# A DoRA forward pass on one core: the end of the first load phase in small pieces, the first stores one chunk earlier, the first block's load in three parts

## The chip, the core and the metric

The kernel runs on one core of one Trainium2 chip. The metric is the device time of one execution in microseconds, taken as the median of several runs; less is better. The profile is that of one further execution. Its engines are called PE (TensorE, matrix products; PEld is its weight load), DVE (VectorE), ACT (ScalarE), POOL (GpSimd) and SP (SyncE, which here only issues DMAs and waits). Data are moved between the chip's large memory (HBM) and the on-chip memory (SBUF) by 16 DMA engines, which work for all queues. SP's DMAs appear as queue q1, ACT's as q10.

## The reference, cut to what matters

```python
batch, seq_len, in_dim, out_dim = 16, 2048, 256, 256      # rank = 16
W_adapted = W + scale * (lora_A @ lora_B)
W_norm = np.sqrt(np.sum(W_adapted ** 2, axis=0, keepdims=True) + 1e-8)
W_final = W_adapted / W_norm * m
y = x.reshape(-1, in_dim) @ W_final                       # 32768 x 256 times 256 x 256
```

The small matrix W_final is made once. The large part is 32,768 rows of x, read as 33.5 MB in float32, multiplied by it, and written as 33.5 MB in float32.

## The kernel before

**Tiling.** The rows are cut into 8 blocks of 4,096 rows (4 MB). In a block each of the 128 partitions holds 32 neighbouring rows, 32 KB in one piece of HBM. A block has 8 chunks of 512 rows (4 rows per partition), 64 chunks in all, numbered g = 0 to 63; two chunks make a pair p = 0 to 31. "Rows 8 to 15 of block 0" are those of each partition: chunks 2 and 3, that is pair 1. There are five buffers for x of a block each (`XBUFS`). The result of a chunk is written over its own x, so a buffer is free for block b + 5 once block b is stored.

**A pair's way.** POOL rounds the pair from float32 to bf16 (`xb`, line 192). PE transposes it by eight products with the identity (line 297, `turned`). DVE copies the transposed pair out of PSUM (`xt`, line 233). PE multiplies by `w_final` in two groups of eight products, one group for each chunk (line 311, `product`). ACT copies each chunk's result into the place of its x (line 251) and, when a store is due, drains and issues it (lines 254 to 260). Semaphores carry these steps: `rounded`, `turned`, `copied`, `room`, `product`. POOL keeps two `xb` buffers, so the cast of pair p waits until pair p - 2 is transposed.

**The beginning.** Before the loop, PE, DVE and ACT make `w_final` from W, A, B and m; the last steps are two products on DVE for `wam` (line 223), a reciprocal (line 226), and two products for `w_final` (line 229). PE transposes pair 0 ahead of it and then waits for `w_final` (line 322).

**Loads.** SP issues them in the order of the list `loads` of (first chunk, number of chunks), line 104: chunks 0 and 1, chunks 2 to 7, then whole blocks 1 to 6, then block 7 in two halves. Each has its semaphore. POOL waits for a pair's load where it differs from that of the pair before (line 182). The first five blocks go at once. Ahead of block 5, SP waits for stores 0, 1 and 2 (lines 159 to 163; `HALF` is 2), ahead of the last half for store 3.

**Stores.** ACT issues them in the order of the list `stores` of (first chunk, number of chunks, chunk after which it is due), lines 112 to 118. Stores 0 and 1 are blocks 0 and 1, due after chunks 22 and 23. Stores 2 and 3 are the halves of block 2, both due after chunk 24. Then come four stores of one chunk each (chunks 24 to 27, due after chunk 27), in which each partition has only 4 KB in one piece. The remaining stores are due after chunk 47 or later.

**The pause.** At pair 15 (`REST`) POOL waits for store 2, line 188, and so all engines behind it stand still while the first stores run. So the order of the large transfers is: loads of five blocks; stores of blocks 0 to 2; loads of blocks 5 to 7, beside the four stores of one chunk; stores of the rest.

Of the kernel before, what the change touches and what calls it, by code (L numbers as in the profile page):

```python
# [11 lines left out]
def kernel(  # L12
# [10 lines left out]
    nc = tc.nc  # L23
# [19 lines left out]
    XBUFS = 5  # L43
    CH = DJ // J
# [56 lines left out]

    units = [(b * CH, CH) for b in range(NBLK - 1)]
    units += [(NCH - CH, CH // 2), (NCH - CH // 2, CH // 2)]
    loads = [(0, 2), (2, CH - 2)] + units[1:]
    load_of = {g: n for n, (g0, cnt) in enumerate(loads) for g in range(g0, g0 + cnt)}


# [1 line left out]

    F = NBLK - XBUFS  # L110
    G = F * CH
    stores = [(b * CH, CH, 22 + b) for b in range(F - 1)]
    stores += [(G - CH, CH // 2, 24), (G - CH // 2, CH // 2, 24)]
    FIRST = len(stores)
    stores += [(G + c, 1, G + 3) for c in range(4)]
# [9 lines left out]
    def sem(name):  # L125
        if name not in sems:
            sems[name] = tc.alloc_semaphore(name)
        return sems[name]
# [50 lines left out]
    ).then_inc(sem("ident"), 1)  # L179
    for p in range(NPR):  # L180
        b, c = divmod(p, PRB)
        if p == 0 or load_of[2 * p - 1] != load_of[2 * p]:
            nc.gpsimd.wait_ge(sem(f"load{load_of[2 * p]}"), 16)
        if p == 0:


            nc.gpsimd.wait_ge(sem("dve"), 4)
        if p == REST:
            nc.gpsimd.wait_ge(sem(f"store{HALF}"), 16)
        if p >= NXB:  # L190
            nc.gpsimd.wait_ge(sem("turned"), p - NXB + 1)
        nc.gpsimd.tensor_copy(  # L192
            out=xb_bufs[p % NXB][:],
            in_=x_bufs[b % XBUFS][:, 2 * c * J : 2 * (c + 1) * J, :],
        ).then_inc(sem("rounded"), 1)
# [51 lines left out]
    for g in range(NCH):  # L247
        b, c = divmod(g, CH)
# [123 lines left out]
```

## Time and profile before

| what | value |
|---|---|
| median of 7 runs | 164.45 us (162.94 to 165.58) |
| time of the profiled execution | 164.19 us |
| its span, first to last instruction | 162.9 us |
| PE busy | 95.7 us (59% of the span) |
| ACT, POOL, DVE busy | 63.9, 63.0, 47.8 us |
| moved by DMA | 67.42 MB, mean 414 GB/s over the span |
| store 0 issued | 51.95 us |
| pair 15's cast after the pause | 78.44 us |
| last store issued | 133.58 us |

The profile has a row of 40 slices for each engine and for the DMA engines, a row for each queue with its share of the 16 engines' time, groups of instructions with their mean length and what ended the idle time before them, and the DMA issues with the time to landing. Stretches of the span can be asked for on their own; they give each engine's busy time, the granted clock, the DMA engines' busy share and their rate. A packet is counted whole in the stretch in which it starts, so in short stretches the share can be over 1.

### The profile page before, as it was taken

How to read it: one execution, taken by the hardware profiler on the slowest of the kernel's cores; microseconds unless marked ns; L12 is line 12 of the kernel's file. 1: busy time of each engine (PE TensorE's matmuls, PEld its weight loads, DVE VectorE, ACT ScalarE, POOL GpSimd, SP SyncE). 2: the span in 40 equal slices, each digit the busy share in tenths (PEclk: the TensorE clock that was granted, in tenths of full speed). 3: DMA queues.
4: the chain of work that ended last, by engine and by line, in shares of the span. 5: the costliest groups of instructions: out<-in, count | busy, mean ns of one | idle time of the engine just before them, and what ended most of it. 6: DMA issues, size and time to landing. Idle time of an engine off the chain costs nothing. (4 is left out here: it accounts for less than half of the span.)

```text
span 162.9 us, 2005 instructions
## 1 busy us (share of the span) xinstructions
PE 95.7 (59%) x786; PEld 84.3 (52%) x786; DVE 47.8 (29%) x44; ACT 63.9 (39%) x67; POOL 63.0 (39%) x39
## 2 busy tenths in 40 slices
PE   0292499999999720000299989999999950000000
PEld 0061489999999610000279979989899930000000
DVE  0419644536353500000033635444444400000000
ACT  3010047686867460000026684865876860000000
POOL 1046367677685000000764469298586200000000
PEclk9999999999999996555558999999999998555555
DMA  4999998999988989999999999899999999999996
GB/s 169 451 447 422 459 443 386 499 402 394 507 386 370 402 386 467 428 390 439 398 388 435 419 450 431 371 420 421 374 422 443 459 443 394 445 451 435 394 426 290
DMA packets 3780, 67.42 MB, mean 414 GB/s; under 512 B 561, under 2 KB 578, under 8 KB 1218
## 3 DMA queue, kind: packets, MB, share of 16 engines
q1 hardware_dynamic: 1584, 33.82, 48.9%
q10 hardware_dynamic: 2194, 33.59, 48.8%
q14 instruction: 2, 0.02, 0.0%
HBM read 33.85 MB, written 33.55 MB: 414 GB/s over the span
## 5 line engine op out<-in xcount | busy, mean ns | idle before, releaser
L251 ACT COPY x_sb<-y_ps 128x1024 f32<-128x1024 f32 x64 | 62.0, 1014 | 60.8 <-PE y_ps L311 60.3
L192 POOL CAST xb<-x_sb 128x2048 bf16<-128x2048 f32 x32 | 60.5, 1902 | 62.5 <-DMA out_dram<-x_sb 26.6
L311 PE MATMUL y_ps<-w_final,xt 128*128 128x256 bf16 x512 | 63.8, 279 | 1.9 <-PEq L286 1.8
L233 DVE COPY xt<-xt_ps 128x1024 f32<-128x1024 f32 x32 | 39.2, 1224 | 72.2 <-PE xt_ps L297 72.2
L311 PEld LDWEIGHTS y_ps<-w_final,xt 128*128 128x128 bf16 x512 | 51.1, 100 | 9.2 <-issue 2.6
L297 PE MATMUL xt_ps<-identity,xb 128*128 128x128 f32 x264 | 37.4, 289 | 27.8 <-PEq L286 27.8
L297 PEld LDWEIGHTS xt_ps<-identity,xb 128*128 128x128 f32 x264 | 32.2, 150 | 30.0 <-issue 29.6
L229 DVE TENSOR_TENSOR w_final<-wam,rnorm 128x256 bf16<-128x256 f32 x2 | 3.7, 1872 | 0.0
L278 PE MATMUL y_ps<-sq,ones 128*128 128x256 f32 x4 | 2.1, 674 | 1.6 <-DVE sq L218 1.6
L243 ACT ACTIVATE norm<-y_ps,eps_col 128x256 f32<-128x256 f32 x1 | 0.5, 474 | 6.3 <-PE y_ps L278 6.3
L267 PE MATMUL y_ps<-identity,a_nat 128*16 128x128 f32 x2 | 0.6, 397 | 4.0 <-DMA a_nat<-in_lora_A_dram 4.0
L278 PEld LDWEIGHTS y_ps<-sq,ones 128*128 128x128 f32 x4 | 1.2, 323 | 2.3 <-DVE sq L218 2.1
L241 ACT ACT_TABLE_LOAD x1 | 1.3, 1283 | 2.4 <-issue 2.4
L267 PEld LDWEIGHTS y_ps<-identity,a_nat 128*16 128x16 f32 x2 | 0.1, 88 | 4.0 <-issue 4.0
L198 POOL MEMSET xb<- 128x2048 bf16 x1 | 1.8, 1805 | 0.7 <-PE xt_ps L297 0.7
L226 DVE RECIPROCAL rnorm<-norm 128x256 f32<-128x256 f32 x1 | 1.7, 1747 | 0.0
L209 DVE CAST b_bf<-b_nat 16x256 bf16<-16x256 f32 x1 | 0.3, 281 | 4.0 <-DMA b_nat<-in_lora_B_dram 4.0
L220 DVE COPY m_all<-y_ps 128x256 f32<-128x256 f32 x1 | 0.4, 425 | 3.3 <-PE y_ps L283 3.3
L271 PE MATMUL y_ps<-b_bf,aT 16*128 16x256 bf16 x2 | 0.6, 403 | 1.3 <-DVE aT L211 1.3
L283 PE MATMUL y_ps<-m_row,ones 1*128 1x256 f32 x2 | 1.2, 710 | 0.0
L271 PEld LDWEIGHTS y_ps<-b_bf,aT 16*128 16x128 bf16 x2 | 0.1, 105 | 1.8 <-DVE aT L211 1.8
L214 DVE SCALAR_TENSOR_TENSOR wa<-y_ps,w_nat 128x512 f32<-128x512 f32 x1 | 0.7, 691 | 0.8 <-PE y_ps L271 0.8
(13 smaller groups left out, 3.7 us busy)
## 6 DMA issues: line engine op xcount, KB each, us to landing
x_sb<-in_x_dram SPq DMA_DIRECT2D x6, 4096.0 KB, 28.8
out_dram<-x_sb ACTq DMA_DIRECT2D x5, 4096.0 KB, 21.0
out_dram<-x_sb ACTq DMA_DIRECT2D x5, 2048.0 KB, 29.3
x_sb<-in_x_dram SPq DMA_DIRECT2D x2, 2048.0 KB, 33.6
x_sb<-in_x_dram SPq DMA_DIRECT2D x1, 3072.0 KB, 11.9
out_dram<-x_sb ACTq DMA_DIRECT2D x4, 512.0 KB, 48.3
x_sb<-in_x_dram SPq DMA_DIRECT2D x1, 1024.0 KB, 5.2
w_nat<-in_W_dram SPq DMA_DIRECT2D x1, 256.0 KB, 2.8
```

Source lines behind the costliest of these rows:

```text
L192: nc.gpsimd.tensor_copy(out=xb_bufs[p % NXB][:], in_=x_bufs[b % XBUFS][:, 2 * c * J : 2 * (c + 1) * J, :],).then_inc(sem("rounded"), 1)
L198: nc.gpsimd.memset(xb_bufs[NPR % NXB][:], 0.0).then_inc(sem("rounded"), 1)
L214: nc.vector.scalar_tensor_tensor(out=wa[:], in0=ab_ps, scalar=float(scale), in1=w_nat[:], op0=ALU.mult, op1=ALU.add).then_inc(dv, 1)
L226: nc.vector.reciprocal(out=rnorm[:], in_=norm[:]).then_inc(dv, 1)
L229: i = nc.vector.tensor_mul(out=w_final[:, t], in0=wam[:, t], in1=rnorm[:])
L233: nc.vector.tensor_copy(out=xt_bufs[p % NXT][:].rearrange("p r t -> p (r t)").bitcast(FP32), in_=xt_ps[p % 2][:],).then_inc(sem("copied"), 1)
L241: nc.scalar.activation(out=warm[:], in_=eps_col[:], func=AF.Sqrt)
L251: nc.scalar.copy(out=x_bufs[b % XBUFS][:, c * J : (c + 1) * J, :], in_=y_ps[g % 2][:]).then_inc(sem("room"), 1)
L278: i = nc.tensor.matmul(n2_ps, ones[:], sq[:, t, :], start=(t == 0), stop=(t == KC - 1))
L283: nc.tensor.matmul(mb_ps, ones[0:1, :], m_row[:], start=True, stop=True).then_inc(pe, 1)
L297: i = nc.tensor.transpose(xt_ps[p % 2][:, j * P : (j + 1) * P], xb_bufs[p % NXB][:, j, :].bitcast(FP32), identity[:],)
L311: i = nc.tensor.matmul(y_ps[h][:, j, :], xt_bufs[p % NXT][:, r : r + P, t], w_final[:, t, :], start=(t == 0 and (j % (J // 2)) == 0), stop ...
```

## The change

Three edits. The list of loads is cut differently: the load of chunks 2 to 7 becomes one of chunks 2 and 3 and one of chunks 4 to 7, and block 4, the last of the first five, becomes one load of its first five chunks and three loads of one chunk each (4 KB in one piece for each partition). Stores 0 and 1 are due one chunk earlier, after chunks 21 and 22. POOL's wait for a load is asked for each chunk of a pair instead of for its first chunk alone, since the boundary between two loads now falls inside pair 18 (chunks 36 and 37) and pair 19.

```diff
     units += [(NCH - CH, CH // 2), (NCH - CH // 2, CH // 2)]
-    loads = [(0, 2), (2, CH - 2)] + units[1:]
+    loads = [(0, 2), (2, 2), (4, CH - 4)] + units[1 : XBUFS - 1]
+    loads += [((XBUFS - 1) * CH, CH - 3)]
+    loads += [(XBUFS * CH - 3 + c, 1) for c in range(3)] + units[XBUFS:]
     load_of = {g: n for n, (g0, cnt) in enumerate(loads) for g in range(g0, g0 + cnt)}
...
-    stores = [(b * CH, CH, 22 + b) for b in range(F - 1)]
+    stores = [(b * CH, CH, 21 + b) for b in range(F - 1)]
     stores += [(G - CH, CH // 2, 24), (G - CH // 2, CH // 2, 24)]
...
         b, c = divmod(p, PRB)
-        if p == 0 or load_of[2 * p - 1] != load_of[2 * p]:
-            nc.gpsimd.wait_ge(sem(f"load{load_of[2 * p]}"), 16)
+        for g in (2 * p, 2 * p + 1):
+            if g == 0 or load_of[g - 1] != load_of[g]:
+                nc.gpsimd.wait_ge(sem(f"load{load_of[g]}"), 16)
         if p == 0:
```

Here CH is 8, XBUFS is 5 and F is 3. What is computed, the number of bytes moved and the order of the loads by address stay the same.

## The prediction

> **What bounds the kernel now.** I read the page first: rows 2 and 3, then the DMA-issuing rows, then half-microsecond windows around the places where loads and stores change over. In the first fence the first two lines are the DMA queues of the page (the third number is the share of 16 engines' span), the third is the list of waits for SP, the rest are windows (window, length, busy time of PE, PEld, DVE, ACT, POOL, granted clock, DMA share, GB/s).
>
> ```profile
> q1 hardware_dynamic: 1584, 33.82, 48.9%
> q10 hardware_dynamic: 2194, 33.59, 48.8%
> ...
> SPq L163 <- DMA out_dram<-x_sb: 74.2, 1, 74.2
> ...
> 50.50:51.00 0.50, 0.50 (x7) 0.44 (x6) 0.50 (x1) 0.17 (x1) 0.50 (x1) 1.00 2.13 918
> 51.00:51.50 0.50, 0.50 (x8) 0.45 (x5) 0.18 (x1) 0.50 (x1) 0.50 (x1) 1.00 0.00 0
> 51.50:52.00 0.50, 0.50 (x7) 0.50 (x6) 0.00 (x0) 0.34 (x1) 0.38 (x1) 1.00 0.02 0
> 52.00:52.50 0.50, 0.50 (x7) 0.48 (x6) 0.00 (x0) 0.14 (x1) 0.00 (x0) 1.00 0.00 0
> 52.50:53.00 0.50, 0.50 (x7) 0.45 (x5) 0.43 (x1) 0.50 (x1) 0.00 (x0) 1.00 2.44 1049
> ...
> 52.00:78.00 26.00, 5.22 (x45) 4.13 (x43) 2.45 (x2) 4.97 (x5) 0.00 (x0) 0.70 0.99 422
> 78.00:86.00 8.00, 5.52 (x26) 4.57 (x27) 1.23 (x1) 1.14 (x2) 5.63 (x3) 0.50 0.99 366
> 86.00:112.00 26.00, 25.13 (x227) 22.99 (x226) 11.12 (x10) 18.15 (x19) 16.90 (x10) 0.99 1.01 430
> 112.00:122.00 10.00, 9.78 (x90) 8.78 (x89) 4.81 (x4) 6.81 (x9) 7.33 (x4) 1.00 0.99 397
> 122.00:161.00 39.00, 10.38 (x96) 9.38 (x93) 3.67 (x3) 8.70 (x10) 3.89 (x3) 0.70 1.01 434
> ```
>
> The two queues fill 97.7% of the engines' time, so the kernel is bound by moving 67.4 MB; PE, the busiest engine, has 59%. What can be won is where the engines stand or run slow. A packet is booked where it starts: the 16 packets of 32 KB of 52.50:53.00 take 2.44 x 0.5 = 1.22 us. The last load packets start at 50.4 to 50.9, so they end at 51.6 to 52.1, on average at 51.85; the first store packets start at 52.8 to 53.0. Between loads and stores every DMA engine stands **1.0 us**. The other two changes of direction (78 to 86, 112 to 122) do not stand, but run at 366 and 397 GB/s against 434: 8 x (1 - 366/434) = 1.25 us and 10 x (1 - 397/434) = 0.85 us lost. They already have small stores (4 KB a row) beside large loads.
>
> The next fence is the timeline of DVE, POOL and ACT (start, length, engine, line, operation).
>
> ```profile
> 11.84 0.76 DVE L223 TENSOR_TENSOR wam<-wa,m_all 128x256 f32<-128x256 f32 x2
> 12.51 1.75 DVE L226 RECIPROCAL rnorm<-norm 128x256 f32<-128x256 f32 x1
> 13.76 3.92 POOL L192 CAST xb<-x_sb 128x2048 bf16<-128x2048 f32 x2 [3.67 <-DMA x_sb<-in_x_dram]
> 14.29 3.67 DVE L229 TENSOR_TENSOR w_final<-wam,rnorm 128x256 bf16<-128x256 f32 x2
> ...
> 48.21 1.93 ACT L251 COPY x_sb<-y_ps 128x1024 f32<-128x1024 f32 x2 [0.69 <-PE y_ps L311]
> 50.83 1.01 ACT L251 COPY x_sb<-y_ps 128x1024 f32<-128x1024 f32 x1 [0.69 <-PE y_ps L311]
> 51.95 0.37 ACTq L145 DMA_DIRECT2D out_dram<-x_sb  x1
> ```
>
> The first store leaves at 51.95, after chunk 22 (copies start with chunk 0 at 22.01 and come two per 2.62 us; 48.21 is chunks 20 and 21). 0.90 us later its first packet starts: the gap is that latency, begun as the loads end. The two w_final products take 3.67 us, where the two wam products of the same size took 0.76: each ends 0.28 us after one of the two POOL casts that started at 13.76.
>
> **The change, part by part.**
>
> *Store 0 due at chunk 21, store 1 at 22.* Nothing is added on ACT; two drains and issues move up. Chunk 21 ends at 50.14, and the present distance from copy to issue is 0.11: 50.25 instead of 51.95. ACT's next copy then comes about 0.5 us later, as it does today at 52.36; queued behind it is PE's "room", then pairs up to 14. Nobody needs those soon: POOL waits 26.6 us at pair 15 for store 2, which hides 0.5 us fully. The two half stores of block 2 stay at chunk 24.
>
> *Rows 8 to 15 on their own.* (2, 6) becomes (2, 2) and (4, 4). Pair 1 need no longer wait for the 3 MB that land at 13.7: (0, 2) landed at 1.4 + 5.2 = 6.6, and 1 MB more at 430 GB/s is 2.4 us, so about 9.0. Its cast follows pair 0's (8.20 + 1.89) at 10.1 to 12.0. That catches wam: it would start at 11.84, is held to about 12.3 and costs 0.2. Pair 2 still waits for the rest of block 0 (13.8) and blocks the first w_final product to about 16.0; the second is then free, 0.4: w_final is ready at 16.4 instead of 17.96, **1.5 us earlier**, and with it all PE work up to chunk 29. On the path to the end this is worth nothing beyond the gap: pair 15 is held by stores. It moves store 0 to about 48.7. If wam were also caught twice, or (2, 2) landed after 12, the gain falls towards 0 and store 0 goes at 50.25.
>
> *The last three chunks of block 4 one by one.* Eight packets of 32 KB per engine (8 x 1.22) become eight of 20 KB and 24 of 4 KB. The trace has 4 KB packets only as stores. Two bounds, from the queue view of single windows (packets, MB, share of 16 engines):
>
> ```profile
> q10 hardware_dynamic: 40, 0.11, 54.0%
> ...
> q1 hardware_dynamic: 32, 0.52, 122.2%
> q10 hardware_dynamic: 32, 0.13, 31.8%
> ...
> q10 hardware_dynamic: 120, 1.43, 100.4%
> ```
>
> The first line is 82:83, stores alone: 15 are semaphore writes, one is a 16 KB packet of about 1.2 us, and (0.54 x 16 - 1.2)/24 = 0.31 us each for 4 KB. The next two are 94:95, beside large loads: 0.318 x 16/32 = 0.159 us each. At 0.159 the new split costs 24 x 0.159 - 3/8 x 8 x 1.22 = 0.16, with three more semaphore writes 0.2 us; at 0.31 another 24 x 0.15 = 3.6. Below nothing is excluded, since the bytes are the same. I take 0.2: the rows alongside another queue are the nearer, and loads of small rows ran at full rate even at the start (the 2 KB rows of W filled the engines at about 0.09 us each between 2.5 and 3.0). Splitting block 0 adds eight packets per engine, about 0.06.
>
> A rule speaks against this edit. The Trainium skill, "DMA: Bandwidth & Descriptors", section "Rules for kernel authors", asks for 1 MiB or more per DMA, and the section on the anatomy of a DMA fits 2.0 us + bytes/436 GB/s. With it three loads of 512 KB cost 3 x 3.2 = 9.6 us instead of 3.7: 6 us more, an estimate from that page, and the kernel would be slower by about 5 us. The rows say no: from 86 to 112 four DMAs of 512 KB flow beside loads at 430 GB/s. The fixed part is latency of one DMA, and here many are queued.
>
> *SP and POOL.* SP issues four more loads, 0.43 us median each, 1.7 us together: it ends its first batch near 6 instead of 4.2 and then waits 74.2 us for stores. If that cover were gone, 1.7 us. Block 1's issue moves from 2.1 to about 2.5, its packets not before 13. POOL gets four more waits, for (4, 4) at pair 2 and for chunks 37, 38, 39 at pairs 18 and 19, behind which all later casts queue. Those pairs run at 87 and 90; the small loads land about 30 us before. Cost nothing; were they late, every microsecond would hit PE, ACT and the 112.20 stores.
>
> *Which queue goes first.* The same page, section "Queues, rings and completion order", says that an engine goes round its queues packet by packet. Loads issued at 78.48 should then appear at 79.4; the last line of the fence, 79:83, has store packets only, and the first load packet starts near 83.2, some five 16 KB and three 4 KB packets later. So a newcomer waits for about eight packets already taken in. By the rule store 0 starts at 48.7 + 0.9 = 49.6; by the trace eight packets of 4 KB later, about 1.3 us, at 50.9. The loads run to about 52.1 (51.85 + 0.26), so both close the gap, and I use the trace.
>
> *Sum.* -1.0 (gap) + 0.2 + 0.06 = **-0.74 us**. After this the order is unchanged: stores 0 to 2 end 0.74 earlier, so pair 15's cast (78.44) and block 5's loads (78.48) start near 77.7, and the last store, now due at the end of the 162.9 us span, lands near 162.15. The profiled execution took 164.19 and becomes 163.45; the median of the seven runs is 0.26 above it: 164.45 - 0.74 = **163.7**.
>
> **The rivals.** About 1% is what a measurement of this kernel can tell from no change (1.64 us; the seven runs span 2.6).
>
> - *Gap closed as above*, chance 0.46: 163.7, its own range 162.5 to 164.9, from a standing time between 0.6 and 1.4 and the spread of the runs.
> - *More than the gap of this execution*, 0.24. How long w_final is held depends on which of DVE and POOL starts first, and the first store moves with it, so slower executions may stand longer than 1.0. The new order has over 3 us in hand. Then the median falls to the two fastest runs (about 163.0) less 0.74: 162.3. For it: runs of 162.94 and 163.06; against: one profile can't show it.
> - *The mixing costs what the standing did*, 0.15. The two existing changeovers lose 0.85 and 1.25 us without standing. Then -0.74 + 1.05 = +0.3: 164.8. Against: between 86 and 112 the mixture ran at 430.
> - *4 KB loads at 0.31 us*, slower, 0.15. For each of the 24 packets per engine at 0.31 instead of 0.159, 0.15 us. All: 164.45 - 0.74 + 3.6 = 167.3. It decides from 16 packets on (16 x 0.15 - 0.74 = 1.66). For it: the 82:83 line; against: that is stores, and only while alone.
> - That the change does not do what it says (store 0 still behind the loads, as the loads were behind stores at 78.5) needs a lag counted in time, 4.7 us: start at 53.4, gap 1.3, time 165.0. It is inside the third case.
>
> **How the numbers follow.** Faster by over 1% (under 162.8): 0.24 x 0.7 + 0.46 x 0.18 = 0.25. Slower by over 1% (above 166.1): 0.15 x 0.9 + 0.15 x 0.1 = 0.15. Within: 0.60. Range 161.9 to 166.0: leaves out the lower fifth of the second case (0.05) and most of the fourth (0.14).
>
> **What would show it.** In the profile after: store 0 issued near 48.7; no half microsecond without packets between 50 and 54 beyond packet length; w_final done near 16.4; pair 15's cast near 77.7; windows 78 to 86 and 112 to 122 as slow as before, 0.7 earlier; span near 162.15. Wrong if q1's 4 KB packets fill far more than 0.16 us each, if a standing time remains near 52, or if POOL waits for a load at pair 18 or 19.

## The result and the profile after

The changed kernel takes 162.46 us (median of 13 runs, 162.25 to 162.68) where the kernel before takes 164.41 (34 runs, 162.94 to 165.58): a ratio of 0.9897, 95% interval 0.987 to 0.9925. The ratio leaves out runs more than 1.5% above the fastest of their kernel, of which the kernel before has some and the changed one none, so it is nearer to 1 than the quotient of the two medians (0.988). The changed kernel is about 1% faster, and its runs spread over 0.43 us where those of before spread over 2.6. The profiled execution took 162.68 us, its span is 161.4: 1.5 less than before.

The queues of the page and the same stretches as before (window, length, busy PE, PEld, DVE, ACT, POOL, clock, DMA share, GB/s), here with 46 to 52 as a whole and in part in place of the half microseconds:

```profile
q1 hardware_dynamic: 2160, 33.82, 49.6%
q10 hardware_dynamic: 2194, 33.59, 48.6%
```

```profile
46.00:52.00 6.00, 5.89 (x55) 5.25 (x53) 3.21 (x3) 4.21 (x5) 3.46 (x2) 1.00 1.00 362
48.00:50.00 2.00, 2.00 (x21) 1.81 (x19) 1.23 (x1) 1.31 (x2) 1.71 (x1) 1.00 0.82 332
50.00:52.00 2.00, 1.90 (x18) 1.55 (x17) 1.12 (x1) 1.41 (x3) 0.18 (x1) 1.00 1.00 262
52.00:78.00 26.00, 3.63 (x32) 2.88 (x30) 1.33 (x2) 3.70 (x4) 0.00 (x0) 0.61 1.01 435
78.00:86.00 8.00, 5.85 (x33) 4.93 (x34) 1.23 (x1) 1.72 (x2) 5.63 (x3) 0.57 1.03 441
86.00:112.00 26.00, 25.34 (x231) 23.09 (x229) 12.24 (x10) 17.65 (x19) 18.03 (x10) 1.00 1.00 427
112.00:122.00 10.00, 9.78 (x90) 8.86 (x88) 4.00 (x5) 7.71 (x8) 6.69 (x5) 1.00 1.03 439
```

Two things are to be seen. First, from 46 to 52 the engines no longer stand (share 1.00), but they move 362 GB/s in place of 434, and from 50 to 52 only 262. That loses 6 x (1 - 362/434) = 1.0 us, as much as the standing cost before: the standing has become slow packets. (Before, 50 to 52 shows 262 GB/s too, at a share of 0.61, but there it says little. The engines work in step, and of each one only the packet that starts in the window is counted.)

Second, the two later changeovers run at 441 and 439 GB/s, where they ran at 366 and 397. Since whole packets are counted where they start, it is safer to divide the rate by the share: 370 and 401 before, 428 and 426 now. By the prediction's formula the loss there was 1.2 and 0.8 us and is 0.1 and 0.2.

The timeline of DVE, POOL and ACT shows the early part and the end of the pause:

```profile
11.19 0.76 DVE L228 TENSOR_TENSOR wam<-wa,m_all 128x256 f32<-128x256 f32 x2
11.87 1.75 DVE L231 RECIPROCAL rnorm<-norm 128x256 f32<-128x256 f32 x1
13.65 2.45 DVE L234 TENSOR_TENSOR w_final<-wam,rnorm 128x256 bf16<-128x256 f32 x2
13.82 2.00 POOL L197 CAST xb<-x_sb 128x2048 bf16<-128x2048 f32 x1 [2.54 <-DMA x_sb<-in_x_dram]
...
48.55 0.37 ACTq L149 DMA_DIRECT2D out_dram<-x_sb  x1
...
78.11 3.74 POOL L197 CAST xb<-x_sb 128x2048 bf16<-128x2048 f32 x2 [27.93 <-DMA out_dram<-x_sb]
82.16 1.90 POOL L197 CAST xb<-x_sb 128x2048 bf16<-128x2048 f32 x1 [0.31 <-PE xt_ps L302]
86.26 1.90 POOL L197 CAST xb<-x_sb 128x2048 bf16<-128x2048 f32 x1 [2.21 <-PE xt_ps L302]
88.91 1.90 POOL L197 CAST xb<-x_sb 128x2048 bf16<-128x2048 f32 x1 [0.75 <-PE xt_ps L302]
```

w_final is ready at 16.1 and store 0 leaves at 48.55, 3.4 us earlier than before. Pair 15 starts at 78.11, only 0.33 earlier than the 78.44 of before. From there to the end of the span it is 83.3 us now and was 84.5. So of the 1.5 us, 0.3 come before pair 15 and 1.2 after it. By the formula the later changeovers lose about 1.6 us less, and part of that goes again at the end: taking each packet over its whole length, the engines are idle for a mean of 0.98 us between 146 and the end of the span before, and for 1.30 now. The casts at 86.26 and 88.91 are pairs 18 and 19: what they waited for is PE, not the small loads.

### The profile page after: what moved, and what is told of

Its sections match the earlier page's. It is cut to its first block, busy times and chain, and to the rows that moved or that the text cites. A ratio compares the mean times of both kernels' runs of the same rounds, so it can differ in the third digit from the quotient of the medians.

```text
span 161.4 us, 2012 instructions
## 1 busy us (share of the span) xinstructions
PE 95.3 (59%) x786; PEld 83.8 (52%) x786; DVE 46.6 (29%) x44; ACT 63.9 (40%) x67; POOL 62.9 (39%) x39
## 3 DMA queue, kind: packets, MB, share of 16 engines
q10 hardware_dynamic: 2194, 33.59, 48.6%
## 5 line engine op out<-in xcount | busy, mean ns | idle before, releaser
L234 DVE TENSOR_TENSOR w_final<-wam,rnorm 128x256 bf16<-128x256 f32 x2 | 2.5, 1266 | 0.0
L288 PEld LDWEIGHTS y_ps<-m_row,ones 1*128 1x128 f32 x2 | 0.5, 306 | 0.7 <-issue 0.7
```

Of the source, the lines that this page charges most:

```text
L234: i = nc.vector.tensor_mul(out=w_final[:, t], in0=wam[:, t], in1=rnorm[:])
L288: nc.tensor.matmul(mb_ps, ones[0:1, :], m_row[:], start=True, stop=True).then_inc(pe, 1)
```

## The experiments

All times with a ratio are medians against the kernel before, run on the same chip; the median of before was 164.41 to 164.64 in the four rounds, so ratios compare better than medians. The other numbers are from one profiled execution of each kernel. "Head" is the start of pair 15's cast, "tail" what is left of the span after it. The columns "78 to 86" and "112 to 122" give GB/s and, in brackets, GB/s divided by the DMA share, which is the figure to compare.

| kernel | store 0 | head | tail | 78 to 86 | 112 to 122 | median | ratio (95%) |
|---|---|---|---|---|---|---|---|
| before | 51.95 | 78.44 | 84.5 | 366 (370) | 397 (401) | 164.4 | 1 |
| changed | 48.55 | 78.11 | 83.3 | 441 (428) | 439 (426) | 162.46 | 0.9897 (0.987, 0.9925) |
| e1 due only | 51.45 | 77.96 | 84.4 | 388 (373) | 407 (399) | 163.22 | 0.9931 (0.9907, 0.9956) |
| e2 block 0 only | 51.60 | 78.08 | 84.4 | 386 (375) | 415 (411) | 163.45 | 0.9953 (0.9934, 0.9972) |
| e3 4 KB loads only | 50.15 | 77.43 | 83.7 | 430 (417) | 417 (409) | 164.48 | 0.9984 (0.9954, 1.0014) |
| e4 due, 4 KB | 50.80 | 77.36 | 84.3 | 397 (382) | 422 (414) | 163.39 | 0.9943 (0.9918, 0.9967) |
| e5 due, block 0 | 48.63 | 77.72 | 83.5 | 463 (429) | 449 (424) | 162.55 | 0.9905 (0.987, 0.994) |
| e6 4 KB, block 0 | 50.32 | 77.36 | 83.7 | 408 (404) | 421 (413) | 163.02 | 0.9946 (0.9917, 0.9974) |
| e7 skew 0.9 us | 51.46 | 79.96 | 83.5 | 412 (389) | 434 (421) | 164.92 | 1.0057 (1.0033, 1.008) |
| e8 late small stores | 48.13 | 77.92 | 83.6 | 463 (429) | 429 (425) | 162.48 | 0.9899 (0.9865, 0.9932) |
| e9 skew 0.45 us | 50.85 | 78.42 | 84.0 | 422 (402) | 435 (418) | 164.19 | 0.9977 (0.9952, 1.0002) |
| e10 e5, early skew | 48.86 | 78.95 | 83.4 | 447 (430) | 450 (425) | 163.80 | 0.9977 (0.9956, 0.9999) |
| e11 due at 18, 19 | 46.51 | 78.30 | 83.5 | 429 (429) | 440 (427) | 163.17 | 0.9917 (0.9887, 0.9947) |
| e12 cast after w_final | 50.77 | 77.62 | 84.7 | 395 (399) | 431 (418) | 163.19 | 0.9939 (0.9914, 0.9965) |

**The three edits apart (e1 to e6).** Each kernel takes one or two of the edits that matter here: the due chunks, block 0 in three loads, the 4 KB loads. POOL's wait for each chunk is in all six. The lists are those of the diff.

```diff
-    stores = [(b * CH, CH, 22 + b) for b in range(F - 1)]
+    stores = [(b * CH, CH, 21 + b) for b in range(F - 1)]
```

> Before with one edit: stores 0 and 1 due after chunks 21 and 22. Gap theory (all of the gain is the standing time near 52 us): store 0 issued near 50.3 instead of 51.95, first packet right after the loads' end at 51.9, so 1.0 us less: 163.4. Lockstep theory (the gain comes from the stretches 78 to 86 and 112 to 122, which run slow while all 16 engines work in step, and small loads beside the first stores take them out of step): the 32 KB loads end first, nothing mixes, the later stretches stay near 366 and 397 GB/s, and the time is 163.4 to 164.0. Both alike here; the rates of the later stretches tell.

```diff
-    loads = [(0, 2), (2, CH - 2)] + units[1:]
+    loads = [(0, 2), (2, 2), (4, CH - 4)] + units[1:]
```

> Before with one edit: block 0 loaded as chunks 0-1, 2-3, 4-7. w_final ready about 1.7 us earlier, store 0 issued near 50.3 with its due chunk unchanged. Gap theory: as e1, 163.4. Lockstep theory: engines stay in step, later stretches slow, 163.4 to 164.0. If the split of block 0 by itself is worth nothing: 164.4.

```diff
-    loads = [(0, 2), (2, CH - 2)] + units[1:]
+    loads = [(0, 2), (2, CH - 2)] + units[1 : XBUFS - 1]
+    loads += [((XBUFS - 1) * CH, CH - 3)]
+    loads += [(XBUFS * CH - 3 + c, 1) for c in range(3)] + units[XBUFS:]
```

> Before with one edit: the last three chunks of block 4 as 4 KB loads, store 0 still issued near 52. Loads end near 52.1, stores start near 52.9. Gap theory: standing 0.8 left, 164.4 (4 KB costs 0.2). Lockstep theory: no mixing with stores, later stretches slow, 164.4. If 4 KB loads by themselves bring the engines out of step: stretches 78 to 86 and 112 to 122 above 420 GB/s and 163.0 or less.

e4 is the due chunks of e1 with the loads of e3, e5 the due chunks of e1 with the loads of e2, e6 both loads with the due chunks of before.

> The changed kernel without the split of block 0: store 0 issued near 50.3. Gap theory: the gap is closed as in e1, 4 KB cost 0.2: 163.6. Lockstep theory: store packets start while about 10 small loads per engine are left, engines fall out of step, 78 to 86 and 112 to 122 above 420 GB/s, 162.5 like the changed kernel.

> The changed kernel without the 4 KB loads: block 4 in one load of 32 KB rows, block 0 in three loads, stores 0 and 1 due at 21 and 22. Store 0 issued near 49. Lockstep theory: about two 32 KB packets per engine are left of the loads when the stores arrive, all are already taken in, nothing mixes, all engines stay within 0.2 us of each other, 78 to 86 stays below 400 GB/s: 163.3, as e1 and e2. Rival, that an early store 0 alone is what counts: as the changed kernel, 162.5.

> The changed kernel with stores 0 and 1 due at 22 and 23 as before: store 0 issued near 50.3, the 4 KB loads in place. Lockstep theory: the stores come late in the small loads, engines get 0.3 to 0.5 us out of step as in e4, later stretches part slow: 163.0 to 163.4. Rival (4 KB loads with an early w_final are enough): 162.5.

e1 and e2 win 0.7% and 0.5% on their own, and together (e5) 0.95%, a little less than the sum. The 4 KB loads win nothing that can be measured in the median in any company: e3 against before 0.9984, e4 against e1 0.9943 to 0.9931, e6 against e2 0.9946 to 0.9953, the changed kernel against e5 0.9897 to 0.9905, each pair inside its intervals. So the expectation that e4 would equal the changed kernel and e5 fall short of it failed both ways: the two edits that count both move store 0. Whether the 4 KB loads steady the time is open. The runs of e5 go from 162.27 to 163.53, four of 13 above 163, while those of the changed kernel end at 162.68 and those of e8, which has the 4 KB loads too, at 163.0.

The profiled execution of e3 was by luck its fastest (162.35 us, in runs from 162.35 to 165.88) and had store 0 at 50.15 although no edit moved it. In e1 and e2 store 0 left at 51.45 and 51.60, later than the 50.3 expected. In e2 `w_final` was ready at 16.36, as early as hoped; the time went in the products behind it. First before, then e2:

```profile
20.35 2.49 PE L311 MATMUL y_ps<-w_final,xt 128*128 128x256 bf16 x16
```

```profile
18.75 3.62 PE L315 MATMUL y_ps<-w_final,xt 128*128 128x256 bf16 x16
```

The 16 products of pair 0 take anything from 2.46 us (e3) to 3.62 us (e1, e2, e7, e10, e11, e12), 2.66 in the profile of the changed kernel; those of the pairs after it take 1.91. So store 0 has a second source of variation, about 1.2 us. The granted clock is 1.00 in all these stretches; what sets the length was not found.

Why store 0 moves in e3 is in its timeline of DVE and POOL:

```profile
13.75 2.45 DVE L234 TENSOR_TENSOR w_final<-wam,rnorm 128x256 bf16<-128x256 f32 x2
13.89 4.07 POOL L197 CAST xb<-x_sb 128x2048 bf16<-128x2048 f32 x2 [4.34 <-DMA x_sb<-in_x_dram]
```

DVE's first product starts 0.14 us ahead of POOL's cast and is not held; before, it started 0.53 behind it, and the two products took 3.67 instead of 2.45. The DVE chain hangs on the landing of lora_B: the cast of lora_B started at 5.25 in the profile of before, at 4.68 here, and anywhere from 3.99 to 5.25 in the fourteen profiles.

**Is it w_final that moves store 0? (e12)** One wait is added to the kernel before, nothing else:

```diff
+        if p == 1:
+            nc.gpsimd.wait_ge(sem("dve"), 8)
```

> Before with one more wait: POOL's cast of pair 1 waits until w_final is made, so that DVE's two products never wait for it. No load and no due chunk is changed. If the place of w_final sets store 0 and store 0 sets the time: w_final takes about 0.8 us instead of 3.7 and is ready near 15, pair 1's cast ends near 17, PE goes on about 1.6 us earlier, store 0 is issued near 50.3, the time is 162.6 to 163.0 and the runs lie closer together than the 2.6 us of before. If not: 164.4, or more by the later cast.

w_final takes 0.76 us in the profile of e12 (13.09 to 13.85), and PE goes on at 16.02 instead of 18.62. That profile alone proves little, since lora_B landed early in it (its cast at 4.02) and w_final took 0.76 us without the wait, too, in the equally early execution of e10. The runs tell: the median is 163.19, ratio 0.9939, a little above the 162.6 to 163.0 expected, and the runs spread over 1.45 us (162.79 to 164.24). So a single wait, which can only delay a cast, brings over half of the gain. The slowness of w_final next to a cast, and its variation, was a good part of what the kernel before paid. The rest of the gain isn't there: the tail of the profiled execution is as long as before.

**Is earlier always better? (e11)** The due chunks of the changed kernel become 18 and 19.

> The changed kernel with stores 0 and 1 due after chunks 18 and 19, three chunks earlier: store 0 issued near 44.7. Time by store 0's issue fell from 164.2 at 51.95 to 162.4 at 50.2 and rose to 162.7 at 48.5 in the executions profiled so far. If it is flat before about 50 (all bytes have to be moved, no engine stands): 162.3 to 162.8. If earlier mixing of loads and stores costs by its length: 163 or more. If it still gains by being earlier: under 162.2.

Store 0 left at 46.51, not near 44.7, since this is one of the executions in which pair 0's products took 3.62 us. The median is 163.17. Earlier mixing seems to cost a little: 0.7 us by the medians, 0.3 by the ratios, whose intervals overlap, while the runs themselves (162.83 to 163.38 against 162.25 to 162.68, in different rounds) do not. Of the profiled executions without a useless load, those of e3 and e6 (store 0 at 50.15 and 50.32; 162.35 and 162.43 us) are the fastest, those at 48.1 to 48.6 take 162.55 to 162.81, those at 50.8 162.96 (e4) and 163.64 (e12), those at 51.5 to 52.0 163.7 to 164.2. So the changed kernel seems to lie not at the optimum but on its safe side, where a shift of w_final by a microsecond costs little; one execution of each kernel can't prove it.

**Why the tail is shorter (e7, e8, e9, e10).** The row of the DMA share in 40 slices of 0.1 us between 58 and 62, while stores alone run. First before, then the changed kernel, each digit the share of packets that start in the slice:

```profile
DMA  0000000009970000000009990000000009990000
```

```profile
DMA  7970070979777970070979977907070799977977
```

Before, all 16 engines start their 32 KB packets within 0.3 us, then none for 0.9. After the change they start at all times: the engines are out of step. The theory to be tried was that engines in step slow each other when all of them change direction at once. e7 takes them out of step without an earlier store, by two loads that nobody uses (bytes are added, nothing is left out); e9 has the first of the two only.

```diff
+        if loads[n][0] == (XBUFS - 1) * CH:
+            nc.sync.dma_start(
+                out=skew[0:8, :], in_=x_flat[0:96, :].rearrange("(p j) k -> p (j k)", p=8)
+            ).then_inc(sem("skewed"), 16)
+            nc.sync.dma_start(
+                out=skew[32:36, :], in_=x_flat[96:144, :].rearrange("(p j) k -> p (j k)", p=4)
+            ).then_inc(sem("skewed2"), 16)
```

> Before, with two loads of no use behind block 4's load: 12 KB for each of 8 partitions, then of 4 partitions, which only 8 and 4 of the 16 engines carry, so that the engines end the loads 0.45 and 0.9 us apart. Due chunks and all other loads as before. Lockstep theory: 78 to 86 above 420 GB/s instead of 366 and 112 to 122 above 420 instead of 397, saves 1.2 to 1.7, costs up to 0.9 on the four engines that end last: 163.3 to 164.2, with the rates of the two stretches as its proof. Rival (it is the early store or the small stores' issue time, not the step): both stretches stay slow and the time rises by up to 0.9, to 165.3.

> Before with one load of no use behind block 4's load: 12 KB for each of 8 partitions, carried by 8 of the 16 engines, so half the engines are 0.45 us behind the others at the first stores (0.6 with the 0.15 that is there). Everything else as before. Lockstep theory (packets of all 16 engines that change direction at the same time are stretched): windows 78 to 86 above 400 GB/s (366 before), 112 to 122 above 420 (397 before), saves 0.8 or more, costs up to 0.45: 163.9. Rival (only an early store 0 helps): the two stretches stay, 164.9.

Here the same windows of e7:

```profile
78.00:86.00 8.00, 4.00 (x19) 3.34 (x20) 1.22 (x1) 0.31 (x1) 5.63 (x3) 0.50 1.06 412
112.00:122.00 10.00, 9.72 (x90) 8.79 (x89) 3.94 (x5) 7.45 (x8) 7.14 (x4) 1.00 1.03 434
```

With store 0 at 51.46 the tail falls to 83.5 us, and 112 to 122 rises from 397 to 434 (for a share of 1 from 401 to 421). 78 to 86 rises to 412, short of the 420 expected, and even that is flattering: for a share of 1 it is 389, and since pair 15 starts 1.5 us later in e7, part of the slow stretch lies behind 86. From 78 to 90 it is 399 against 391 before. In e9 the tail is 84.0, the rates 402 and 418 for a share of 1. So the rival, that only an early store helps the later stretches, is refuted for the second of them, as far as one profile each can do that, while the first recovers by half in e9 and hardly in e7. The rival was right about the total, since the useless loads cost what they bring: e7 was expected at 163.3 to 164.2 and took 164.92, slower than before, and e9 was expected at 163.9 and took 164.19.

e10 puts the load of e9 behind block 1 in the kernel of e5, so that the engines are out of step before the first stores come.

> The kernel of e5 (no 4 KB loads, early stores) with the load of no use behind block 1's load: half the engines are 0.45 us behind through the whole load phase. Lockstep theory: the packets near 50 to 52, which are stretched in e5 (46 to 52 runs at 366 GB/s), are stretched less, above 390 GB/s, which pays for the 0.45: 162.3 to 162.6. Rival (the first changeover costs its 0.7 us in any case): 46 to 52 as in e5, time 162.55 + 0.45 = 163.0.

Four windows of e10, and the row of slices from 58 to 62:

```profile
22.00:25.00 3.00, 3.00 (x30) 2.79 (x28) 1.44 (x2) 2.31 (x3) 0.71 (x1) 1.00 0.91 208
50.00:52.00 2.00, 2.00 (x19) 1.65 (x17) 0.81 (x1) 1.47 (x2) 0.50 (x1) 1.00 0.84 360
78.00:86.00 8.00, 5.01 (x28) 4.26 (x29) 1.23 (x1) 1.22 (x2) 5.62 (x3) 0.56 1.04 447
112.00:122.00 10.00, 9.79 (x90) 8.84 (x89) 4.15 (x4) 7.39 (x8) 6.85 (x4) 1.00 1.06 450
```

```profile
DMA  9970997000079990997000009990999000009990
```

All three changeovers are now nearly free of slow packets: 50 to 52 moves 360 GB/s in a share of 0.84, which is 428 for a share of 1, where e5 and the changed kernel moved 262 in a share of 0.96 and 1.00. That agrees with the theory. The time was expected at 162.3 to 162.6 and is 163.80, for a reason that it did not hold: the odd load itself, meeting 16 engines in step, made a slow stretch of its own. From 22 to 25 the engines are busy 0.91 of 3 us and move 208 GB/s; the same bytes at 434 need 1.44 us, so 1.3 us went there. The head of e10 is 1.2 us later than that of e5, and its median 1.25 us. The slow packets were moved, not removed.

Last, the rival that the issue time of the small stores governs the stretch 78 to 86:

```diff
-    stores += [(G + c, 1, G + 3) for c in range(4)]
+    stores += [(G + c, 1, G + 5) for c in range(4)]
```

> The changed kernel with the four stores of one chunk due after chunk 29 instead of 27, so issued some 2 us later, near 60 as in the kernel before. Lockstep theory: no change, 162.5, 78 to 86 above 430 GB/s. Rival (the slow stretches hang on when the small stores are issued: 57.6 in the changed kernel, 60.06 before): 78 to 86 falls to about 390 and the time is 163.3.

It did not do what was meant: chunk 29 comes out only after the pause, since PE multiplies pair 14 after turning pair 15, and the stores left at 85.43. So it doesn't try an issue near 60. It shows that 78 to 86 runs fast (463) with no small store in flight, and that issuing them 28 us later costs nothing (162.48).

What is shown and what stays open. In the three profiles in which the first stores run in step (before, e1, e2) the stretch 78 to 86 moves 370 to 375 GB/s for a share of 1. In all that are more or less out of step it moves more, but by very different amounts: 382 in e4, 389 to 404 in e7, e12, e9 and e6, 417 in e3, and 428 to 430 in the changed kernel, e5, e8, e10 and e11. So being out of step goes with faster changeovers, but what decides between a part and the whole was not found, nor what in the memory or the engines makes the packets slow. Out of step also has a price: the engines end at different times. By their packets they are idle for a mean of 0.98 us after 146 before, 1.84 in e12 and 2.01 in e7. That goes some way to explain why e12 has the longest tail, 84.7, although both its later changeovers run faster than before.

## Why the prediction came out as it did

The direction was right and the time lies in the stated range; the size was too small, 0.74 us of 164.45 against a measured 1.0% (0.75 to 1.3%). The mechanism was right in the smaller part only. Of the 1.5 us in the profile, the term that was to bring all of it brought 0.3, and a term put at 0 brought 1.2. That the time came out so near was luck in that sense. By its steps:

- **w_final and store 0: right.** 16.4 and 48.7 were forecast, 16.1 and 48.55 came, and in e2, whose chain ran nearly as late as that of before, w_final was ready at 16.36. wam was not held: it started at 11.19, 0.10 us before pair 1's cast ended, and took its 0.76. That pair 0's products can take 1.2 us more or less was not in the forecast of store 0.
- **SP, POOL, small loads: right.** Pairs 18 and 19 did not wait for loads. The 4 KB loads bring and cost nothing measurable in the median (e5 beside the changed kernel), so the rule that speaks against small DMAs did not decide, as was argued from the rows. They are the part of the change that could be left out, if the spread of the runs of e5 is no sign against it.
- **The gap term, -0.74: too large.** In the head it came to -0.33. The step "eight packets of 4 KB later, about 1.3 us, at 50.9" failed: between 48.6 and 52.4 the trace has packets of q1 alone, as the fence below shows, and q10 begins only after that. The lag, 3.9 us here, does not go by the number of packets: it is 3.6 with 32 KB packets in e5 (48.63 to about 52.2), with 32 packets started in that time instead of 347. So the rival of the 4.7 us lag had the right kind of delay. What it missed is that the loads would be stretched until then: 1.0 us lost from 46 to 52. Where store 0 left at 50.2 to 50.8 beside 4 KB loads (e3, e4, e6), 46 to 52 ran at 402 to 416 GB/s, the first stores started as the loads ended, and the head fell by 1.0 to 1.1 us. There the gap closed as the sum had it.
- **Two readings of the skill.** The prediction set the trace against the rule of going round packet by packet. In the Trainium skill, "DMA: Bandwidth & Descriptors", section "Queues, rings and completion order", a packet is a group of about 9 to 17 descriptors, while the profile counts each semaphore write of 4 bytes as a packet of its own. So the count of eight does not test that rule, and no run here does. And the fit of 2.0 us plus the bytes stands in the section "Anatomy of one DMA — SWDGE (gpsimd) path", for DMAs that GpSimd issues; the loads here are issued by SP.
- **"After this the order is unchanged": failed, and this is the larger error.** The term for the later changeovers was put at 0, "windows 78 to 86 and 112 to 122 as slow as before". The tail measured 1.2 us less. The view was at hand, the loss of 1.25 and 0.85 us was worked out, but it was taken as a fixed price of a changeover.
- **The second case named the other half.** "How long w_final is held depends on which of DVE and POOL starts first, and the first store moves with it": e3 and e12 show that. Its 162.3 was nearer to the result than the 163.7 chosen, but it too put the later changeovers at 0. It was given 0.24 because one profile can't show it; the spread of the seven runs was the evidence and was under-read.
- **4 KB loads at 0.31 us: did not happen.** Packets of 4 KB kept 0.16 us except in the slow stretch, where the 32 KB packets of e5 slowed down as well (262 GB/s from 50 to 52 in both).

The queue view of the changed kernel between 48.6 and 52.4 (packets, MB, share of 16 engines); there is no line for q10:

```profile
q1 hardware_dynamic: 347, 1.27, 101.2%
```

## What to carry to other kernels

When one kernel's runs spread by 1.6% while its profile shows a cause that can fall either way (here: which of two engines starts first), price the change against the spread and not against the one execution profiled. Where the DMA engines are full, a stretch with share 1 and a low rate is as much a loss as one where they stand, and it can appear or vanish far from the edit: compare rates window by window to the end of the span, each divided by its share, since a window of a few packet lengths can be 8% off otherwise (463 for 429 in e5). Issuing the first store some microseconds ahead of the end of the loads closed the gap and absorbed jitter here; going two microseconds earlier still (e11) won nothing more.

## What was not expected of the hardware

- A DMA issued while all engines have work for the other queue shows its first packet 3.5 to 4.9 us later (stores 48.55 to 52.5; loads 78.48 to about 83.3 before, 78.15 to about 81.7 after), whether 4 KB or 32 KB packets are ahead of it; with idle engines it is 0.9. Where the other queue runs out sooner, it comes then: in e3, e4 and e6 1.2 to 2.0 us after the issue. Whether the lag goes by time or by bytes is not separated here.
- One load of 96 KB on 8 engines, put among 32 KB packets of 16 engines in step, cost about 1.3 us of all engines' time (e10, 22 to 25).
- Sixteen engines that start together stay together for tens of microseconds, and the same bytes then move at 370 to 375 GB/s for a share of 1 from 78 to 86, where loads and stores change over, instead of 428 to 430 in the fastest kernels.
